# Two layers of a hybrid encoder on one core: the seven products of a pair of FFN slices are spread over a block of four slices

## The chip, the core and the metric

The kernel runs on one core of a Trainium2 chip. The core has a matrix engine (TensorE: PE for its matmuls, PEld for the loads of its stationary operand), VectorE (DVE), ScalarE (ACT), GpSimd (POOL) and SyncE (SP, which here only issues DMAs). Each engine works off its own queue in order. The metric is the device time of one execution in microseconds; lower is better. "us" is microseconds throughout.

## What is computed

Two layers, each of a half-step SwiGLU feed-forward network (FFN), a mixer, and a second FFN, on 256 tokens of width 1024 with `D_FF = 2816`:

```python
def swiglu(u, w_in, w_out):
    gate, up = jnp.split(u @ w_in, 2, axis=-1)
    return (jax.nn.silu(gate) * up) @ w_out

for l in range(DEPTH):
    h = swiglu(rmsnorm(x, ffn1_pre_g[l]), ffn1_w_in[l], ffn1_w_out[l])
    x = x + 0.5 * rmsnorm(h, ffn1_post_g[l])
    h = hybrid_mixer(rmsnorm(x, mix_pre_g[l]), ...)
    x = x + rmsnorm(h, mix_post_g[l])
    h = swiglu(rmsnorm(x, ffn2_pre_g[l]), ffn2_w_in[l], ffn2_w_out[l])
    x = x + 0.5 * rmsnorm(h, ffn2_post_g[l])
```

There are four FFNs, called FFN 1 to 4 here in order of time (layer 0: 1 and 2; layer 1: 3 and 4). FFN 2 is followed at once by FFN 3.

## The kernel before

**Precision.** Every fp32 operand is split into a high part (a cast to fp32r on ACT) and a low part (the remainder, a subtraction on DVE), and every product is three matmuls, hi·hi, lo·hi and hi·lo (`mm3`, L386 to L388). Each matmul is 128 x 128 by 128 x 512.

**Weights.** All weights come in one stream of units of 128 x 1024 in the order in which they are used (`Stream`). For each unit ACT writes `whi` (L153) and DVE writes `wlo` (L154). There are `WBUFS = 8` such pairs of buffers, so the splitting runs at most eight units ahead of the matmuls: unit n can be written when PE has read unit n - 8 for the last time. SP loads the raw weights, two units (1 MB) at a time into three `raw` buffers.

**FFN.** The inner width is cut into `NS = 11` slices of 256 columns. A *plain* slice is projected for both token blocks (`fin`, 2 x 24 matmuls on 4 units), passes silu and a product (`gate_up`, ACT L441, DVE L442), is transposed and split (`ftr`, L453, L371 and L372) and multiplied with its rows of the output weights (`fout`, 2 x 12 matmuls on 2 units). So PE stays 12 matmuls on every unit.

**Groups.** In FFN 2, 3 and 4 the slices (2, 3) and (6, 7) are projected as a *group* with seven products, P1 to P7, in place of eight (a Strassen-like scheme over token blocks and halves of the contraction). Each product is 12 matmuls on 2 units, so PE stays 6 matmuls on a unit. The operands of the products are made on DVE from the raw weights (`Stream.part`): for each group three subtractions or additions per quarter ahead of P6 (L175 to L177) and one ahead of P4 (L179), 16 in all of 128 x 512; and their results are combined on DVE (L487, L491, L492, L495, L496, L501, L512), 7 of 128 x 512. The raw weights of a group are eight loads of 0.5 MB into `gw` tiles (pool `spl`, 7 buffers) and `w4` tiles, which stay occupied until P5 and P4 have been split. A group's order in the code is

```python
product(s, "P1", lambda ps: act.copy(u, ps))
product(s, "P3", lambda ps: act.copy(v, ps))
product(s, "P2", first)
fout(s - 1, 0); fout(s - 1, 1)
product(s, "P6", sixth)
ftr(s, 0)
product(s, "P7", lambda ps: dve.tensor_add(w, u, ps))
product(s, "P5", fifth)
product(s, "P4", fourth)
fout(s, 0)
```

The results of projections and products go through two PSUM buffers (`psin`): a product can start when the one two before it has been read out. The accumulators of the output are `psacc`. The order on each engine is set by the scheduler of the framework when the kernel is built; it starts from the order of the code.

Of the kernel before, what the change touches and what calls it, by code (L numbers as in the profile page):

```python
# [53 lines left out]
P1 = _snap(TWO_PI, 2.0 ** -10)  # L54
P2 = _snap(TWO_PI - P1, 2.0 ** -23)
# [21 lines left out]


PRODUCTS = (("P1", 2), ("P3", 0), ("P2", 3), ("P6", 2), ("P7", 0), ("P5", 1), ("P4", 3))
GROUPS = (2, 6)  # L80


def ffn_plan(groups):

    r, s = [], 0
    while s <= NS:
        if s in groups:
            r += [("g1", s), ("out", s - 1), ("g2", s), ("out", s)]
            s += 2
            continue  # L90
        if s < NS:
            r.append(("in", s))
        if s >= 1:
            r.append(("out", s - 1))
        s += 1
    return r


MIXER_UNITS = 152
SIZE = {"in": 4, "out": 2, "g1": 6, "g2": 8}  # L100


def stream_plan():

    r = []
    for l in range(L):
        for f in range(2):
            for k, _ in ffn_plan(GROUPS if (l, f) != (0, 0) else ()):
                if k in ("in", "out"):
                    r += [None] * SIZE[k]  # L110
                else:
                    r += [(n, q, h) for n, q in (PRODUCTS[:3] if k == "g1" else PRODUCTS[3:]) for h in range(2)]
            if f == 0:
                r += [None] * MIXER_UNITS
    return r
# [89 lines left out]
def trunk_kernel(ctx: ExitStack, tc: tile.TileContext, x_in, pos, gains, gain0, par, id_in, consts, gw, w, out):  # L205
# [214 lines left out]
    def ffn(l, kpost, after, turn, during=None, start=False, fast=False):  # L420


        ui, uo, hT = {}, {}, {}
        groups = () if start else GROUPS
        for k, s in ffn_plan(groups):
            us = st.take(SIZE[k])
            if k == "out":
                uo[s] = us
            else:
                ui[s] = ui.get(s, []) + us  # L430
        acc = [ps_acc() for _ in range(NTB)]

        def fin(s, tb, turn=None):
            gate_up(s, tb, [inproj(ui[s], tb, turn)])

        def gate_up(s, tb0, pss):
            for tb, ps in enumerate(pss, tb0):
                t = tok()
                with tc.high_priority(offset=CHAIN_LEAD if s == NS - 1 else 0):
                    if fac[tb] is None:  # L440
                        act.activation(t[:, 0:256], ps[:, 0:256], AF.Silu)  # L441
                        dve.tensor_mul(t[:, 256:512], ps[:, 256:512], t[:, 0:256])  # L442
                    else:
                        act.activation(t[:, 0:256], ps[:, 0:256], AF.Silu, scale=fac[tb])
                        dve.scalar_tensor_tensor(t[:, 256:512], ps[:, 256:512], fac[tb], t[:, 0:256],
                                                 op0=ALU.mult, op1=ALU.mult)
                hT[(s, tb)] = t

        def ftr(s, tb):
            t = hT[(s, tb)]  # L450
            pt = ps_tr()
            for i in range(2):
                pe.transpose(pt[:, i * P:(i + 1) * P], t[:, 256 + i * P:256 + (i + 1) * P], ident)  # L453
            hl = tp.tile([P, 2, 256], F32R, tag=("tmp", "tok")[tb], name=nm("hl"), bufs=(TMP, TOK)[tb])
            with tc.high_priority(offset=CHAIN_LEAD if s == NS - 1 else 0):
                split(hl[:, 0, :], hl[:, 1, :], pt[:, 0:256])
            hT[(s, tb)] = hl

        def fout(s, tb, ns=(0, 1)):
            hl = hT[(s, tb)]  # L460
            outproj(acc[tb], [(hl[:, 0, c * P:(c + 1) * P], hl[:, 1, c * P:(c + 1) * P]) for c in range(2)],
                    uo[s], s == 0, s == NS - 1, ns)

        def product(s, n, use):

            ps = ps_in()
            i = [k for k, _ in PRODUCTS].index(n)
            us = ui[s][2 * i:2 * i + 2]
            for p in range(4):
                h, lo = st.get(us[p // 2])  # L470
                c = slice((p % 2) * 512, (p % 2 + 1) * 512)
                if n in ("P1", "P2", "P4"):
                    tb, k = {"P1": (0, 0), "P2": (0, 1), "P4": (1, 1)}[n]
                    ah, al = uh[tb][:, 2 * p + k, :], ul[tb][:, 2 * p + k, :]
                else:
                    k = ("P7", "P3", "P6", "P5").index(n)
                    ah, al = [v[:, k, p % 2, :] for v in sums[p // 2]]
                mm3(ps, ah, al, h[:, c], lo[:, c], p == 0, p == 3)
            use(ps)
            st.done(us)  # L480

        def group(s):

            (u, v), (z, w) = halves(w4()), halves(w4())

            def first(ps):
                dve.tensor_add(z, u, ps)  # L487
                gate_up(s, 0, [z])

            def sixth(ps):  # L490
                dve.tensor_add(u, u, ps)  # L491
                dve.tensor_add(v, v, u)  # L492

            def fifth(ps):
                dve.tensor_add(v, v, ps)  # L495
                dve.tensor_add(u, w, ps)  # L496
                gate_up(s + 1, 0, [v])
                gate_up(s + 1, 1, [u])

            def fourth(ps):  # L500
                dve.tensor_add(w, w, ps)  # L501
                gate_up(s, 1, [w])

            product(s, "P1", lambda ps: act.copy(u, ps))
            product(s, "P3", lambda ps: act.copy(v, ps))
            product(s, "P2", first)
            fout(s - 1, 0)
            fout(s - 1, 1)
            st.done(uo[s - 1])
            product(s, "P6", sixth)  # L510
            ftr(s, 0)
            product(s, "P7", lambda ps: dve.tensor_add(w, u, ps))  # L512
            product(s, "P5", fifth)
            product(s, "P4", fourth)
            fout(s, 0)
            ftr(s + 1, 0)
            ftr(s + 1, 1)
            ftr(s, 1)
            fout(s, 1)
            st.done(uo[s])  # L520

        st.fill()
        if start:
            gate_up(0, 0, inproj2(ui[0]))
            st.done(ui[0])
            fin(1, 0)
            ftr(0, 0)
        else:
            fin(0, 0)
            fin(1, 0, turn)  # L530
            ftr(0, 0)
            fin(0, 1)
            st.done(ui[0])
        ftr(1, 0)
        fin(1, 1)
        ftr(0, 1)
        st.done(ui[1])
        fout(0, 0)
        fout(0, 1)
        ftr(1, 1)  # L540
        st.done(uo[0])
        s = 1
        while s < NS - 2:
            s += 1
            if s == 4 and during is not None:
                during()
            if s in groups:
                group(s)
                s += 1
                continue  # L550
            fin(s, 0)
            fin(s, 1)
            st.done(ui[s])
            fout(s - 1, 0)
            ftr(s, 0)
            fout(s - 1, 1)
            ftr(s, 1)
            st.done(uo[s - 1])
        e = NS - 1

        def tail(tb):
            fin(e, tb)
            fout(e - 1, tb, (0,))
            ftr(e, tb)
            fout(e - 1, tb, (1,))

        tail(0)
        fout(e, 0)
        with tc.high_priority(offset=CHAIN_LEAD):
            post(0, acc[0], l, kpost, 0.5)  # L570
            turn = after(0)
        tail(1)
        st.done(ui[e])
        st.done(uo[e - 1])
        fout(e, 1, (0,))
        if turn is not None:
            turn()
        fout(e, 1, (1,))
        st.done(uo[e])
        with tc.high_priority(offset=CHAIN_LEAD):  # L580
            post(1, acc[1], l, kpost, 0.5, fast)
            return after(1)
# [516 lines left out]
    return list(wm.reshape(-1, P, D))  # L1099


def _ffn_units(w_in, w_out, groups):
    r = []
    o = _out_units(w_out)

# [1 line left out]
        c = np.arange(s * 256, (s + 1) * 256)  # L1107
        return np.concatenate([c, DFF + c])

    for k, s in ffn_plan(groups):  # L1110
        if k == "in":
            r += _in_units(w_in, cols(s))
        elif k == "out":
            r += o[2 * s:2 * s + 2]
        elif k == "g1":
            b = [w_in[:, cols(s + n)].reshape(KD, P, 512) for n in range(2)]
            for c in range(0, KD, 2):
                r += [np.concatenate([b[1][c + 1], b[1][c]], axis=1),
# [54 lines left out]
def _layout(i):  # L1173
    a = {n: np.asarray(v) for n, v in i.items()}
    units = []
    for l in range(L):
        units += _ffn_units(a["ffn1_w_in"][l], a["ffn1_w_out"][l], GROUPS if l > 0 else ())
        units += _mixer_units(a["w_mix_in"][l], a["w_lru_out"][l], a["w_ret_out"][l], a["w_sc_out"][l],
                              a["w_mix_out"][l])
        units += _ffn_units(a["ffn2_w_in"][l], a["ffn2_w_out"][l], GROUPS)  # L1180
    gains = [a[n][l] for l in range(L) for n in ("ffn1_pre_g", "ffn1_post_g", "mix_pre_g", "mix_post_g",
                                                 "ffn2_pre_g", "ffn2_post_g")]
    gains = np.stack([np.broadcast_to(g, (P, D)) for g in gains])
# [33 lines left out]
```

## Time and profile before

| | |
|---|---|
| time, median of 3 runs | 1685.47 us (1685.13 to 1686.81) |
| the profiled execution: its time, its span | 1687.89 us, 1686.1 us |
| PE busy, matmuls | 1658.7 us (98%), 7577 |
| PEld busy | 1361.0 us (81%) |
| DVE busy | 1205.7 us (72%) |
| ACT busy | 910.1 us (54%) |
| DMA, mean | 184 GB/s |

Busy time counts an engine's instructions from start to end; matmuls overlap one another, so a PE that is busy all the time can still be slower than it could be. Better are the starts of successive matmuls and the granted clock of TensorE. FFN 2 lies at 655 to 847 us of the span, FFN 3 at 847 to 1037, FFN 4 at 1491 to 1679.

### The profile page before, as it was taken

What the parts mean: (1) busy time and instruction counts of PE and PEld (TensorE: products, weight loads), DVE (VectorE), ACT (ScalarE), POOL (GpSimd) and SP (SyncE); (2) the same over time, 40 slices, a digit from 0 to 9 for tenths busy, and PEclk for the clock granted to TensorE, in tenths of its full rate; (3) what the DMA queues carried; (4) which work ended last, traced back from release to release, by engine and by line L of the source; (5) the groups of instructions that cost most, each with busy time, mean ns of one, the idle gap of its engine ahead of it and who ended that gap; (6) DMA issues with size and microseconds to landing.
All of it is one profiled execution on the core that took longest, in us unless ns stands there. A gap on an engine that the chain in (4) does not pass through costs nothing.

```text
span 1686.1 us, 19900 instructions
## 1 busy us (share of the span) xinstructions
PE 1658.7 (98%) x7577; PEld 1361.0 (81%) x7577; DVE 1205.7 (72%) x1629; ACT 910.1 (54%) x1335; POOL 65.0 (4%) x110
## 2 busy tenths in 40 slices
PE   9999999999999999999999999999999999999998
PEld 7888788888888887787787887888888888877886
DVE  6655669956656657978598866799666556589783
ACT  6444577644545455656465545766445445466552
POOL 0300100000000001000000001000000000010000
PEclk9999999999999999999999999999999999999999
DMA  8554454555444556446456164545554444745341
GB/s 309 209 196 178 175 187 166 210 186 200 169 180 160 184 220 219 148 182 212 163 199 213 75 233 167 203 171 200 194 189 166 172 178 164 260 175 182 131 175 50
DMA packets 48623, 309.86 MB, mean 184 GB/s; under 512 B 5520, under 2 KB 5904, under 8 KB 15376
## 3 DMA queue, kind: packets, MB, share of 16 engines
q1 hardware_dynamic: 46224, 301.18, 48.9%
q10 hardware_dynamic: 2304, 7.41, 1.3%
q8 instruction: 59, 0.97, 0.2%
q14 instruction: 36, 0.29, 0.0%
HBM read 307.52 MB, written 1.05 MB: 183 GB/s over the span
## 4 chain that ended last, share of the span: by engine, by line
PE 88%; DVE 8%; issue 1%; DMA 1%; POOL 1%; ACT 1%; DVEq 0%; POOLq 0%; ACTq 0%
PE psin L386 20%; PE psin L387 20%; PE psin L388 20%; PE psacc L388 8%; PE psacc L387 8%; PE psacc L386 8%; DVE wlo L154 5%; PE pstr L453 1%; PE pstr L696 1%; DMA raw<-in_w_dram 1%; PE pstr L348 1%; POOL small L292 1%; PE pstr L861 1%; DVE gw L176 0%; DVE gw L175 0%
## 5 line engine op out<-in xcount | busy, mean ns | idle before, releaser
L154 DVE TENSOR_TENSOR wlo<-raw,whi 128x1024 fp32r<-128x1024 f32 (+1 forms) x522 | 625.3, 1215 | 289.9 <-ACT whi L153 278.6
L153 ACT CAST whi<-raw 128x1024 fp32r<-128x1024 f32 (+1 forms) x522 | 536.3, 1049 | 250.2 <-PE psacc L388 128.0
L386 PE MATMUL psin<-whi,uh 128*128 128x512 f32 x1480 | 584.3, 395 | 1.9 <-ACT whi L153 1.4
L388 PE MATMUL psin<-whi,ul 128*128 128x512 f32 x1480 | 578.6, 391 | 2.2 <-DVE ul L372 2.2
L387 PE MATMUL psin<-wlo,uh 128*128 128x512 f32 x1480 | 580.0, 392 | 0.4 <-DVE wlo L154 0.4
L388 PEld LDWEIGHTS psin<-whi,ul 128*128 128x128 f32 x1480 | 278.2, 188 | 60.4 <-DVE ul L372 3.1
L386 PEld LDWEIGHTS psin<-whi,uh 128*128 128x128 f32 x1480 | 278.4, 188 | 57.7 <-ACT whi L153 1.8
L387 PEld LDWEIGHTS psin<-wlo,uh 128*128 128x128 f32 x1480 | 278.4, 188 | 55.7 <-DVE wlo L154 1.1
L386 PE MATMUL psacc<-whi,hl 128*128 128x512 f32 x352 | 141.3, 403 | 9.1 <-ACT whi L153 9.1
L388 PE MATMUL psacc<-whi,hl 128*128 128x512 f32 x352 | 137.6, 394 | 1.0 <-DVE hl L372 1.0
L387 PE MATMUL psacc<-wlo,hl 128*128 128x512 f32 x352 | 137.1, 391 | 0.0
L386 PE MATMUL psacc<-whi,spl 128*128 128x512 f32 x256 | 100.1, 391 | 0.0
L388 PE MATMUL psacc<-whi,spl 128*128 128x512 f32 x256 | 99.6, 389 | 0.0
L387 PE MATMUL psacc<-wlo,spl 128*128 128x512 f32 x256 | 99.6, 389 | 0.0
L292 POOL TENSOR_SCALAR small<-small 128x1 f32<-128x1 f32 x39 | 27.5, 705 | 1568.2 <-ACT w L287 1567.5
L386 PEld LDWEIGHTS psacc<-whi,hl 128*128 128x128 f32 x352 | 66.3, 189 | 23.4 <-ACT whi L153 10.4
L154 DVE TENSOR_TENSOR wlo<-gw,whi 128x512 fp32r<-128x512 f32 x120 | 76.8, 681 | 9.5 <-ACT whi L153 9.2
L388 PEld LDWEIGHTS psacc<-whi,hl 128*128 128x128 f32 x352 | 66.0, 188 | 17.8 <-DVE hl L372 4.2
L153 ACT CAST whi<-gw 128x512 fp32r<-128x512 f32 x120 | 68.0, 620 | 22.2 <-DVE gw L179 9.7
L387 PEld LDWEIGHTS psacc<-wlo,hl 128*128 128x128 f32 x352 | 66.3, 188 | 12.8
L371 ACT CAST hl<-pstr 128x256 fp32r<-128x256 f32 x88 | 32.5, 370 | 69.4 <-PE pstr L453 69.3
L684 ACT COPY tok<-psin 128x512 f32<-128x512 f32 x40 | 23.5, 587 | 62.6 <-PE psin L388 62.6
(191 smaller groups left out, 1645.8 us busy)
## 6 DMA issues: line engine op xcount, KB each, us to landing
raw<-in_w_dram SPq DMA_DIRECT2D x259, 1024.0 KB, 4.9
gw<-in_w_dram SPq DMA_DIRECT2D x36, 512.0 KB, 7.0
w<-in_w_dram SPq DMA_DIRECT2D x12, 512.0 KB, 4.7
gain<-in_gains_dram ACTq DMA_DIRECT2D x10, 512.0 KB, 4.5
w<-in_gw_dram ACTq DMA_DIRECT2D x4, 512.0 KB, 3.4
x<-in_x_dram SPq DMA_DIRECT2D x2, 512.0 KB, 4.9
raw<-in_w_dram SPq DMA_DIRECT2D x4, 256.0 KB, 6.0
out_dram<-x SPq DMA_DIRECT2D x4, 256.0 KB, 2.0
```

Of the source, the lines that this page charges most:

```text
L153: nc.scalar.copy(hi[:, k:k + n], raw)
L154: nc.vector.tensor_sub(lo[:, k:k + n], raw, hi[:, k:k + n].bitcast(F32))
L292: first_e.tensor_scalar(r, ss[:, 0:1], more, EPS / (f * f), op0=ALU.add, op1=ALU.add)
L348: pe.transpose(pt[:, i * P:(i + 1) * P], t[:, c * P:(c + 1) * P], ident)
L371: act.copy(h, src)
L386: pe.matmul(ps, lhsT=xh, rhs=wh, start=first, stop=False)
L387: pe.matmul(ps, lhsT=xh, rhs=wl, start=False, stop=False)
L388: pe.matmul(ps, lhsT=xl, rhs=wh, start=False, stop=last)
L453: pe.transpose(pt[:, i * P:(i + 1) * P], t[:, 256 + i * P:256 + (i + 1) * P], ident)
L684: act.copy(t, ps)
L696: pe.transpose(pt[:, i * SEQ + tb * P:i * SEQ + (tb + 1) * P], toks[tb][:, c * P:(c + 1) * P], ident)
L861: pe.transpose(pt[:, i * P:(i + 1) * P], qk[:, i * P:(i + 1) * P], ident)
```

## The change

Slices 2 to 5 and 6 to 9 become blocks (a, b, c, d). Slices a and b are projected plainly, c and d with the seven products, and the products stand between the steps of a and b. There are still two groups of seven products in each of FFN 2, 3 and 4, so the number of instructions on every engine stays as it was. What moves is the order, that of the weights in the stream with it. `during` (one load of a gain) moves from ahead of slice 4 to ahead of slice 6 in FFN 3.

```diff
-GROUPS = (2, 6)
+SLOT = dict(PRODUCTS)
+BLOCKS = ((2, 3, 4, 5), (6, 7, 8, 9))
...
-        if s in groups:
-            r += [("g1", s), ("out", s - 1), ("g2", s), ("out", s)]
-            s += 2
+        block = [b for b in blocks if b[0] == s]
+        if block:
+            a, b, c, d = block[0]
+            r += [("in", a), ("P1", c), ("out", a - 1), ("P3", c), ("P2", c), ("in", b), ("P6", c), ("out", a),
+                  ("P7", c), ("out", b), ("P5", c), ("P4", c), ("out", c)]
+            s += 4
             continue
...
-            product(s, "P1", lambda ps: act.copy(u, ps))
-            product(s, "P3", lambda ps: act.copy(v, ps))
-            product(s, "P2", first)
-            fout(s - 1, 0)
-            fout(s - 1, 1)
-            st.done(uo[s - 1])
-            product(s, "P6", sixth)
-            ftr(s, 0)
-            product(s, "P7", lambda ps: dve.tensor_add(w, u, ps))
-            product(s, "P5", fifth)
-            product(s, "P4", fourth)
-            fout(s, 0)
-            ftr(s + 1, 0)
-            ftr(s + 1, 1)
-            ftr(s, 1)
-            fout(s, 1)
-            st.done(uo[s])
+            fin(a, 0)
+            fin(a, 1)
+            st.done(ui[a])
+            product(c, "P1", lambda ps: act.copy(u, ps))
+            fout(a - 1, 0)
+            ftr(a, 0)
+            fout(a - 1, 1)
+            ftr(a, 1)
+            st.done(uo[a - 1])
+            product(c, "P3", lambda ps: act.copy(v, ps))
+            product(c, "P2", second)
+            fin(b, 0)
+            fin(b, 1)
+            st.done(ui[b])
+            product(c, "P6", sixth)
+            fout(a, 0)
+            ftr(b, 0)
+            fout(a, 1)
+            ftr(b, 1)
+            st.done(uo[a])
+            product(c, "P7", lambda ps: dve.tensor_add(w, u, ps))
+            ftr(c, 0)
+            fout(b, 0)
+            fout(b, 1)
+            st.done(uo[b])
+            product(c, "P5", fifth)
+            product(c, "P4", fourth)
+            fout(c, 0)
+            ftr(d, 0)
+            ftr(d, 1)
+            ftr(c, 1)
+            fout(c, 1)
+            st.done(uo[c])
...
-            if s == 4 and during is not None:
+            if s == (4 if start else 6) and during is not None:
                 during()
-            if s in groups:
-                group(s)
-                s += 1
+            if any(b[0] == s for b in blocks):
+                block(*range(s, s + 4))
+                s += 3
                 continue
```

The built programs show where things stand. In the rows below the number right behind `whi` or `wlo` is that of the weight unit; `s_` tiles are the summed activations, `hl_` is a slice ready for its output product. All rows are of the first group or block of FFN 2.

On PE of the kernel before, the end of P7 (units 238 and 239) and what follows: two matmuls of the output product of slice 2 (unit 244), then P5 (units 240 and 241).

```order
L386 MATMUL psin_491_5743<-whi239_5637,s_459_5385 128x512
L387 MATMUL psin_491_5743<-wlo239_5638,s_459_5385 128x512
L388 MATMUL psin_491_5743<-whi239_5637,s_460_5386 128x512
L386 MATMUL psacc_444_5307<-whi244_5729,hl_490_5740 128x512
L386 MATMUL psacc_445_5308<-whi244_5729,hl_490_5740 128x512
L386 MATMUL psin_492_5767<-whi240_5660,s_455_5369 128x512
```

On PE of the changed kernel, the end of P7 (units 248 and 249): a transposition and the output product of slice 3 (unit 250) follow.

```order
L389 MATMUL psin_505_5947<-wlo249_5853,s_459_5385 128x512
L390 MATMUL psin_505_5947<-whi249_5852,s_460_5386 128x512
L452 MATMUL pstr_506_5971<-ident_70,tok_495_5777 128x128 x2
L388 MATMUL psacc_444_5307<-whi250_5860,hl_502_5910 128x512
L389 MATMUL psacc_444_5307<-wlo250_5861,hl_502_5910 128x512
```

Between P7 and P5 there were two matmuls, and P5 followed P6 after 12 matmuls of P7 and these; now 24 matmuls of slice 2's output, P7 and 24 of slice 3's output lie between P6 and P5.

On DVE of the kernel before, the combination after P6 (L491, reading `psin_488`) and what stands around it: the operands of P4 are made (L179) and split (units 242 and 243) ahead of it.

```order
L179 TENSOR_TENSOR w4_471_5461<-w4_471_5461 128x512
L154 TENSOR_TENSOR wlo242_5699<-gw_467_5447,whi242_5698 128x512
L154 TENSOR_TENSOR wlo242_5699<-gw_469_5451,whi242_5698 128x512
L179 TENSOR_TENSOR w4_473_5465<-w4_473_5465 128x512
L154 TENSOR_TENSOR wlo243_5707<-w4_471_5461,whi243_5706 128x512
L491 TENSOR_TENSOR w4_482_5577<-w4_482_5577,psin_488_5712 128x512
L154 TENSOR_TENSOR wlo244_5730<-raw119_5727,whi244_5729 128x1024
```

On DVE of the changed kernel the same combination (L489, reading `psin_500`):

```order
L181 TENSOR_TENSOR w4_479_5525<-w4_479_5525 128x512
L156 TENSOR_TENSOR wlo250_5861<-raw124_5858,whi250_5860 128x1024
L441 TENSOR_TENSOR tok_499_5843<-psin_498_5818,tok_499_5843 128x256
L156 TENSOR_TENSOR wlo251_5865<-raw124_5858,whi251_5864 128x1024
L489 TENSOR_TENSOR w4_482_5573<-w4_482_5573,psin_500_5868 128x512
L156 TENSOR_TENSOR wlo252_5884<-gw_472_5505,whi252_5883 128x512
```

It now stands behind the splits of slice 3's output weights (units 250 and 251), and P4's splits (units 254 and 255) come after it.

On SP of the changed kernel, the loads of the second block's products (into the buffers that P5 and P4 of the first block give free); `raw127` holds units 260 and 261, the last ahead of P1 of the second block (units 262 and 263), `raw132` units 264 and 265:

```order
L136 DMA raw127_6032<-in_w_dram 128x2048
L170 DMA gw_514_6061<-in_w_dram 128x1024
L170 DMA gw_515_6063<-in_w_dram 128x1024
L170 DMA gw_516_6065<-in_w_dram 128x1024
L170 DMA gw_517_6073<-in_w_dram 128x1024
L170 DMA w4_518_6075<-in_w_dram 128x1024
L170 DMA gw_519_6077<-in_w_dram 128x1024
L170 DMA w4_520_6079<-in_w_dram 128x1024
L136 DMA raw132_6129<-in_w_dram 128x2048
```

On SP of the kernel before, the same seven loads stand between `raw121` (units 248 and 249) and `raw122` (units 250 and 251), four pairs of plain weights ahead of P1 of the second group (units 258 and 259):

```order
L134 DMA raw121_5788<-in_w_dram 128x2048
L168 DMA gw_512_5991<-in_w_dram 128x1024
...
L168 DMA w4_518_6009<-in_w_dram 128x1024
L134 DMA raw122_5815<-in_w_dram 128x2048
L134 DMA raw123_5867<-in_w_dram 128x2048
```

The loads now come last ahead of the P1 that needs them. Between P4 of one group and P1 of the next lie the weights of one output slice and one plain slice (6 units), where there were two plain slices and three output slices (14 units).

## Rows read from the trace of the kernel before

**Rows 1.** The page: busy time, share of the span, instructions by engine.

```profile
PE 1658.7 (98%) x7577; PEld 1361.0 (81%) x7577; DVE 1205.7 (72%) x1629; ACT 910.1 (54%) x1335; POOL 65.0 (4%) x110
```

**Rows 2.** Waits of PE over the span: total us, times, longest us.

```profile
PE psacc L386 <- ACT whi L153: 9.1, 3, 3.1
...
PE pstr L453 <- DVE tok L442: 2.1, 2, 1.1
...
PE pstr L453 <- DVE hl L372: 0.7, 1, 0.7
```

**Rows 3.** Timeline of PE: P6 to P7's end in group 1, FFN 2, then the clock.

```profile
701.73 0.39 PE L388 MATMUL psin<-whi,s 128*128 128x512 f32 x1
...
704.71 0.39 PE L388 MATMUL psin<-whi,s 128*128 128x512 f32 x1
708.16 0.73 PE L386 MATMUL psacc<-whi,hl 128*128 128x512 f32 x2 [3.06 <-ACT whi L153]
...
711.08 0.63 PE L388 MATMUL psin<-whi,s 128*128 128x512 f32 x1
711.51 0.63 PE L386 MATMUL psin<-whi,s 128*128 128x512 f32 x1
```

**Rows 4.** Timeline of PE: first and last matmul of P6, group 2, FFN 2.

```profile
769.85 0.39 PE L386 MATMUL psin<-whi,s 128*128 128x512 f32 x1
...
772.34 0.39 PE L388 MATMUL psin<-whi,s 128*128 128x512 f32 x1
```

**Rows 5.** Busy time by stretch: two groups of FFN 2, 3 and 4.

```profile
core 0: us, PE busy (x) PEld busy (x) DVE busy (x) ACT busy (x) POOL busy (x), PEclk, DMA share, GB/s
...
688.40:719.10 30.70, 27.01 (x112) 21.47 (x111) 30.70 (x49) 17.38 (x28) 0.00 (x0) 0.94 0.53 189
759.00:784.00 25.00, 25.00 (x111) 20.26 (x110) 25.00 (x40) 16.10 (x26) 0.00 (x0) 1.00 0.63 214
879.20:910.00 30.80, 27.61 (x110) 21.79 (x109) 30.80 (x49) 17.36 (x28) 0.00 (x0) 0.89 0.57 192
950.30:975.40 25.10, 25.10 (x112) 20.30 (x111) 25.10 (x40) 16.32 (x28) 0.00 (x0) 1.00 0.27 90
1524.20:1555.00 30.80, 27.66 (x110) 21.82 (x109) 30.80 (x49) 17.37 (x28) 0.00 (x0) 0.89 0.54 191
1595.20:1620.40 25.20, 25.20 (x112) 20.38 (x111) 25.20 (x40) 16.35 (x28) 0.00 (x0) 1.00 0.27 89
```

**Rows 6.** The same columns: plain slice 4, entry of FFN 2, group 1 with its backlog.

```profile
739.20:756.10 16.90, 16.90 (x79) 13.89 (x78) 12.31 (x22) 8.04 (x17) 0.00 (x0) 1.00 0.13 53
655.90:682.00 26.10, 25.17 (x117) 20.54 (x118) 22.67 (x39) 15.98 (x31) 2.95 (x4) 1.00 0.67 236
682.00:720.90 38.90, 35.21 (x151) 28.23 (x150) 38.87 (x60) 23.81 (x40) 0.00 (x0) 0.96 0.46 167
```

**Rows 7.** Timeline of DVE: three shapes back to back, the combination L491.

```profile
650.19 5.76 DVE L154 TENSOR_TENSOR wlo<-raw,whi 128x1024 fp32r<-128x1024 f32 x5
...
682.98 2.49 DVE L154 TENSOR_TENSOR wlo<-gw,whi 128x512 fp32r<-128x512 f32 x4
...
708.79 0.67 DVE L491 TENSOR_TENSOR w<-w,psin 128x512 f32<-128x512 f32 x1
...
724.07 0.75 DVE L372 TENSOR_TENSOR hl<-pstr,hl 128x256 fp32r<-128x256 f32 x2
...
774.73 0.67 DVE L491 TENSOR_TENSOR w<-w,psin 128x512 f32<-128x512 f32 x1
```

**Rows 8.** Timeline of ACT: the cast of unit 244, and a wait behind group 2.

```profile
705.34 1.17 ACT L153 CAST whi<-gw 128x512 fp32r<-128x512 f32 x2 [1.45 <-DVE gw L179]
...
707.07 1.99 ACT L153 CAST whi<-raw 128x1024 fp32r<-128x1024 f32 x2
...
786.65 2.00 ACT L153 CAST whi<-raw 128x1024 fp32r<-128x1024 f32 x2 [2.86 <-DMA raw<-in_w_dram]
```

**Rows 9.** A stretch in which the DMA engines are nearly full (columns of Rows 5).

```profile
710.00:712.00 2.00, 2.00 (x8) 1.53 (x7) 2.00 (x4) 1.69 (x3) 0.00 (x0) 0.60 0.93 295
```

More of the change, by code (lines that the diff above doesn't have):

```diff
@@ L79, with ffn_plan @@
 PRODUCTS = (("P1", 2), ("P3", 0), ("P2", 3), ("P6", 2), ("P7", 0), ("P5", 1), ("P4", 3))
-GROUPS = (2, 6)
-def ffn_plan(groups):
+SLOT = dict(PRODUCTS)
+BLOCKS = ((2, 3, 4, 5), (6, 7, 8, 9))
+def ffn_plan(blocks):
     r, s = [], 0
     while s <= NS:
-        if s in groups:
-            r += [("g1", s), ("out", s - 1), ("g2", s), ("out", s)]
-            s += 2
+        block = [b for b in blocks if b[0] == s]
[4 more added lines that the diff above has]
+            s += 4
             continue
@@ L99 @@
 MIXER_UNITS = 152
-SIZE = {"in": 4, "out": 2, "g1": 6, "g2": 8}
+SIZE = {"in": 4, "out": 2}
 def stream_plan():
@@ L107, in stream_plan @@
         for f in range(2):
[L108 to L112, printed above, removed]
+            for k, _ in ffn_plan(BLOCKS if (l, f) != (0, 0) else ()):
+                r += [(k, SLOT[k], h) for h in range(2)] if k in SLOT else [None] * SIZE[k]
             if f == 0:
@@ L420, in ffn @@
     def ffn(l, kpost, after, turn, during=None, start=False, fast=False):
[L423 to L430, printed above, removed]
+        ui, uo, up, hT = {}, {}, {}, {}
+        blocks = () if start else BLOCKS
+        for k, s in ffn_plan(blocks):
+            us = st.take(SIZE.get(k, 2))
+            {"in": ui, "out": uo}.get(k, up)[(k, s) if k in SLOT else s] = us
         acc = [ps_acc() for _ in range(NTB)]
@@ L466, in product @@
             ps = ps_in()
-            i = [k for k, _ in PRODUCTS].index(n)
-            us = ui[s][2 * i:2 * i + 2]
+            us = up[(n, s)]
             for p in range(4):
@@ L480, in product, with block, second @@
             st.done(us)
-        def group(s):
+        def block(a, b, c, d):
             (u, v), (z, w) = halves(w4()), halves(w4())
-            def first(ps):
+            def second(ps):
                 dve.tensor_add(z, u, ps)
-                gate_up(s, 0, [z])
+                gate_up(c, 0, [z])
             def sixth(ps):
@@ L496, in fifth @@
                 dve.tensor_add(u, w, ps)
-                gate_up(s + 1, 0, [v])
-                gate_up(s + 1, 1, [u])
+                gate_up(d, 0, [v])
+                gate_up(d, 1, [u])
             def fourth(ps):
                 dve.tensor_add(w, w, ps)
-                gate_up(s, 1, [w])
-            product(s, "P1", lambda ps: act.copy(u, ps))
-            product(s, "P3", lambda ps: act.copy(v, ps))
-            product(s, "P2", first)
-            fout(s - 1, 0)
-            fout(s - 1, 1)
-            st.done(uo[s - 1])
-            product(s, "P6", sixth)
-            ftr(s, 0)
-            product(s, "P7", lambda ps: dve.tensor_add(w, u, ps))
-            product(s, "P5", fifth)
-            product(s, "P4", fourth)
-            fout(s, 0)
-            ftr(s + 1, 0)
-            ftr(s + 1, 1)
-            ftr(s, 1)
-            fout(s, 1)
-            st.done(uo[s])
+                gate_up(c, 1, [w])
+            fin(a, 0)
[31 more added lines that the diff above has]
+            st.done(uo[c])
         st.fill()
@@ L1099, in _out_units, with _ffn_units @@
     return list(wm.reshape(-1, P, D))
-def _ffn_units(w_in, w_out, groups):
+def _ffn_units(w_in, w_out, blocks):
     r = []
@@ L1108, in cols @@
         return np.concatenate([c, DFF + c])
-    for k, s in ffn_plan(groups):
+    for k, s in ffn_plan(blocks):
         if k == "in":
@@ L1114, in _ffn_units @@
             r += o[2 * s:2 * s + 2]
-        elif k == "g1":
+        elif k == "P1":
             b = [w_in[:, cols(s + n)].reshape(KD, P, 512) for n in range(2)]
@@ L1176, in _layout @@
     for l in range(L):
-        units += _ffn_units(a["ffn1_w_in"][l], a["ffn1_w_out"][l], GROUPS if l > 0 else ())
+        units += _ffn_units(a["ffn1_w_in"][l], a["ffn1_w_out"][l], BLOCKS if l > 0 else ())
         units += _mixer_units(a["w_mix_in"][l], a["w_lru_out"][l], a["w_ret_out"][l], a["w_sc_out"][l],
                               a["w_mix_out"][l])
-        units += _ffn_units(a["ffn2_w_in"][l], a["ffn2_w_out"][l], GROUPS)
+        units += _ffn_units(a["ffn2_w_in"][l], a["ffn2_w_out"][l], BLOCKS)
     gains = [a[n][l] for l in range(L) for n in ("ffn1_pre_g", "ffn1_post_g", "mix_pre_g", "mix_post_g",
```

## The prediction

> **What bounds the kernel now.** I read the page first. PE is busy 98% of the span [rows 1], so the question is not which engine is the bound on the whole, but where PE runs below its pace. Its pace is 11 starts from 769.85 to 772.34 us, 0.2264 us for a matmul of 512 columns [rows 4]; the change removes no matmul, so only lost time can come back. The list of PE's waits comes next: the largest is three waits of 3.1 us, 9.1 us in all, each for a weight cast of ACT ahead of an output product [rows 2]. The timeline shows the first of them: P7 starts its last matmul at 704.71, the next one starts at 708.16, and some 2 us later matmuls start every 0.43 us in place of 0.23 [rows 3]. The granted clock is 0.94, 0.89 and 0.89 over the three stretches with such a wait and 1.00 over the three without [rows 5]: after the wait TensorE runs for some microseconds at 1.2 GHz in place of 2.4. So the wait is paid about twice.
>
> All three sit in the first group of their FFN, between P7 and P5. Who is late there? ACT's cast of unit 244 (707.07) comes directly after casts that waited for DVE's L179 [rows 8], and DVE is busy 38.87 of 38.90 us from 682.0 to 720.9 [rows 6]. It makes up a backlog: P6 starts its last matmul at 701.73 [rows 3], and DVE reads its result at 708.79 [rows 7], 7.1 us later. In the second group P6 starts its last matmul at 772.34 [rows 4] and is read at 774.73 [rows 7], 2.4 us later, and PE does not wait there, though DVE is busy all of these 25.0 us too [rows 5]. So inside a group DVE is the bound, and the look-ahead of eight units covers that once, unless DVE comes in late. It does at an FFN's entry, where it is busy 22.67 of 26.10 us [rows 6].
>
> **What DVE has to do, and PE in that time.** Prices by shape are 5.76/5 = 1.15 us for 1024 columns, 2.49/4 = 0.62 for 512 and 0.75/2 = 0.37 for 256 [rows 7]. A group needs 28 half-unit splits, 16 operand steps and 7 combinations, 51 x 0.62 = 31.6; four splits of output units, 4.6; eight of 256 columns, 3.0: 39.2 us. PE needs 132 matmuls x 0.2264 = 29.9, and four pairs of transpositions at 0.3 (an estimate: the 25.00 us of FFN 2's second group less 109 x 0.2264 leave 0.3 for its one pair [rows 5]), 31.1 us. DVE falls 8.1 us behind in every group, and gains in plain slices, where it is busy 12.31 of 16.90 us [rows 6].
>
> A block of four has the same 51 steps (31.6), 16 splits of plain units (18.4) and 16 of 256 columns (5.9): 55.9 us. PE has 276 matmuls (62.5) and eight pairs (2.4): 64.9 us. DVE is at 86% over the block and no longer behind. That an average fits does not say that its parts do, so I took the two halves from the order of the changed kernel. From the start of P1 to that of P6, PE has 108 matmuls and two pairs, 25.1 us; the DVE instructions from the first split of P2's units to the last of P6's are 5 of 1024, 20 of 512 and 4 of 256 columns, 5.8 + 12.4 + 1.5 = 19.7 us. From P6 to the P1 of the next block PE has 174 matmuls and six pairs, 41.2 us; DVE 9, 26 and 8, 10.4 + 16.1 + 3.0 = 29.5 us. Both fit, by 5 and by 11 us.
>
> The place of the wait itself: P5 writes the PSUM buffer that P6 wrote, so it needs the combination after P6. Between P6's last split and that combination stand 15 DVE instructions before (14 x 0.62 + 0.37 = 9.1 us) and 13 now (3 x 1.15 + 8 x 0.62 + 2 x 0.37 = 9.2 us). From P6's start to P5's PE had 24 matmuls (5.4 us) and the two that were pulled forward; now it has 72 and three pairs, 17.2 us. The need is the same and the time three times as long. What is late next there is nothing by the same count: P7 has 62 matmuls (14 us) after its buffers come free for 4.4 us of splits and operand steps, P4 has 50 (11.3 us) for some 3 us.
>
> **Part by part.** (1) The three waits and the slow stretches behind them go. The first and the second group of an FFN hold the same matmuls. In FFN 2 the second takes 25.00 us for 111, so the 112 of the first should take 25.2 us and took 30.7: 5.5 us. In FFN 3, 110 x 25.10/112 = 24.7 against 30.8: 6.1 us; in FFN 4, 110 x 25.20/112 = 24.8 against 30.8: 6.0 us [rows 5]. Together 17.6 us. (2) Matmuls, splits and operand steps: none added or removed, 0. (3) The wait of 0.7 us behind group 2 of FFN 2 [rows 2]: ACT's in-order queue stood 2.86 us at 786.65 for a raw load [rows 8], which was queued behind six loads of product weights for FFN 3. The same six loads stand now behind P4 of FFN 2's second block, ahead of the weights of the output product of slice 9, whose cast stands on ACT ahead of the silu of P5. By the stretch with 295 GB/s [rows 9], five of them that wait for P4's splits and the raw pair behind them are 3.7 MB, 12.4 us; PE has 58 matmuls, 13.1 us, until it needs that silu's turn. That is a margin of nothing. I take the 0.7 us as it is now (net 0), with bounds of 0 and of ACT's whole 2.9 us. (4) Between the blocks, seven loads follow raw127 on SP, and raw132 waits behind them. Six wait for P4's splits and are 3.1 MB, 10.7 us at 295 GB/s; the last is cast on ACT ahead of the silu after P4, and from P4's splits to P4's end PE has 60 matmuls and two pairs, 14.2 us. Covered by 3 us; if that cover went, the silu and the transposition behind it would wait for the rest, three times, 0 to 2.9 us each by the ACT row. (5) Ends of FFNs: two waits for `tok`, 2.1 us [rows 2], stand in the same order of instructions now as before: 0. (6) The load of a gain ahead of slice 6 is on ACT's queue, used after slice 10: 0.
>
> Sum: 17.6 us. The profiled execution took 1687.9 us, which makes 1670.3; it stands 2.4 us above the median of the runs, 1685.5, so the forecast for the median is **1668**.
>
> One rule bears on the size. By busy time alone PE lost 30.7 - 27.0 = 3.7, 3.2 and 3.1 us in the three stretches, 10.0 us [rows 5]. The Trainium skill (Perfetto Trace Analysis, Identifying the Most-Contended Engine) says that matmul busy time does not tell the distance to the limit, and to look at the busy share of weight loads. In the plain slice that is 13.89/16.90 = 82% [rows 6], in the three stretches 70, 71 and 71% [rows 5]: by it 4.6, 4.2 and 4.2 us are lost, 13 us in all, 1672 for the median. The trace agrees that busy time says too little; the count of starts, which I use, sees the slow clock whole.
>
> A second one bears on the range. The slow clock lasts longer after the second and third wait than after the first, though the waits are alike (6.1 and 6.0 against 5.5 us lost). The Trainium skill (TensorE: Matmul & The Clock Gate, Part 1: The HAM clock gate) calls the number of slow matmuls variable from run to run; no run here shows that yet. By it the three would lose 16.5 to 18.3 us, 1667 to 1669.
>
> **The rivals.** *Small waits remain or come up* (the DMA margins of 3 and 4, or a chain of add, silu and transposition that is short by little). For it: the margin in (3) is nil, and DVE enters the first block as late as before. Against it: the halves of the block fit by 5 and 11 us. Price: waits like the 0.7 to 1.1 us that the trace has elsewhere [rows 2], after which the clock stayed at 1.00, in six blocks, 4 to 7 us; up to half the gain, 9 us. It gives 1672 to 1677.
>
> *The wait moves with the products* in the first block of each FFN, because the backlog comes from the entry. Then the same 5.5 to 6.1 us stay and the time is 1685. Against it: a plain slice now stands between entry and P1, with 4 units in 10.9 us of PE, about 3 us of free DVE.
>
> *Slower:* the look-ahead. While PE works on a plain slice it holds its four units 10.9 us long, so DVE may split only four units ahead and the operand steps of P6 (12 x 0.62 = 7.4 us, with P6's and the plain slice's splits 14.5 us) come too late in all six blocks. It decides from the point where they don't start before P3's end: PE has 60 matmuls there, 13.6 us, less than 14.5. Then each block pays a wait with a slow clock, 5.8 us x 6 = 35, less 17.6: 1703. Against it: the operand steps need only splits of P3 and P2, and no free unit buffer, so they can run while PE is still on P1 to P2.
>
> That the change does not do what it says is excluded by the order of the built program.
>
> **How the numbers follow.** Forecast (all three waits gone, no new one above 1 us each) 0.68; small waits 0.18; wait moved 0.06; slower 0.08. A measurement of this kernel can tell about 0.2%, 3.4 us, from no change. Faster 0.86, same 0.06, slower 0.08. The range goes from 1664 (18.3 us, the 0.7 us and the spread of the runs shown, 1.7 us) to 1677 (small waits at their largest) and leaves out the two last rivals.
>
> **What would show it.** In the trace after: no wait of PE for a weight cast of 3 us; granted clock 1.00 from 650 to 1680; DVE with gaps inside the blocks, about 86% busy; the combination after P6 read within 3 us of P6's last start. Step (3) is wrong if PE waits at the end of FFN 2 for the silu after P5; step (4) if it does so between blocks in all three FFNs. The forecast is wrong if a wait long enough to lower the clock appears in any block; its place (ahead of P6, or ahead of P5) would tell the look-ahead from the backlog.

## The result, and the profile after

The changed kernel takes 1666.37 us (median of 4 runs, 1666.25 to 1666.93). Beside it the kernel before took 1685.89 us (1685.13 to 1686.81): a ratio of 0.9885, 95% interval 0.9867 to 0.9902. That is 19.5 us or 1.15% less, far over the 0.2% that a measurement here can tell. The forecast was 1668, the range 1664 to 1677.

The page of after, busy time by engine (answers to [rows 1]) and the shares of the chain of work that ended last; below it the span with its mean granted clock:

```profile
PE 1646.6 (99%) x7577; PEld 1356.3 (81%) x7577; DVE 1204.4 (72%) x1629; ACT 914.0 (55%) x1335; POOL 65.0 (4%) x110
...
PE 92%; DVE 3%; ACT 1%; issue 1%; DMA 1%; POOL 1%; DVEq 0%; POOLq 0%; ACTq 0%
```

```profile
core 0: 1664.4 us, clock 0.998
```

The numbers of instructions are those of before, on every engine; the span is 21.7 us shorter than the 1686.1 us of before. The largest waits of PE in after (total us, times, longest us; answers to [rows 2]):

```profile
PE psin L388 <- ACT whi L155: 2.3, 1, 2.3
PE psin L390 <- DVE ul L374: 2.2, 2, 1.1
PE pstr L452 <- DVE tok L441: 2.0, 2, 1.0
```

The three waits for a weight cast ahead of an output product, 9.1 us in [rows 2], are gone from the list, and so is the 0.7 us for `hl`; the two of 1.0 us for `tok` at the ends of FFNs are left. The first row is the start of the program.

The blocks by stretch (columns of [rows 5]): FFN 2's first and second block, the first block of FFN 3 and of FFN 4, then the two halves of FFN 2's first block, P1 to P6 and P6 to the next P1:

```profile
684.50:747.10 62.60, 62.60 (x286) 51.64 (x284) 53.41 (x81) 37.74 (x62) 0.00 (x0) 1.00 0.55 201
747.10:812.00 64.90, 64.90 (x295) 53.19 (x293) 55.10 (x83) 38.25 (x60) 0.00 (x0) 1.00 0.52 187
868.10:931.40 63.30, 63.30 (x288) 52.22 (x287) 54.10 (x82) 37.71 (x62) 0.00 (x0) 1.00 0.55 199
1506.50:1569.80 63.30, 63.30 (x288) 52.22 (x287) 54.11 (x82) 37.71 (x62) 0.00 (x0) 1.00 0.55 198
695.80:720.70 24.90, 24.90 (x114) 20.53 (x112) 24.83 (x39) 15.45 (x25) 0.00 (x0) 1.00 0.36 127
720.70:762.00 41.30, 41.30 (x189) 33.76 (x188) 31.61 (x49) 24.53 (x42) 0.00 (x0) 1.00 0.63 229
```

PE has no gap in any of them and the granted clock is 1.00 throughout, where [rows 5] has 0.94, 0.89 and 0.89. DVE is busy 85% of a block.

**Where the time came from.** I laid the starts of all matmuls of the two traces side by side. The region that the change orders anew begins with the first matmul of slice 2 and holds 552 matmuls of 512 columns and 16 pairs of transpositions in both (in before it ends at the first matmul of slice 10). That region took 136.5, 136.1 and 136.1 us in FFN 2, 3 and 4 and takes 129.35, 129.34 and 129.37: 20.6 us. The way to the first of them took 1.0 us less, and each of the stretches between and behind them stands within 0.15 us. Against 0.2266 us for an undisturbed start, the 20.6 us are, roughly: 13.8 us of starts over 0.25 us late (the waits of [rows 2], which count idle time alone, and the late starts directly behind them), 5.0 us of starts at the slow clock, 1.2 us of slightly late starts just behind transpositions and 1.1 us of them elsewhere, less 0.5 us that transpositions take longer.

### The profile page after: what moved, and what is told of

Same layout as the page of the kernel before. It is cut to its first block, busy times and chain, and to the rows that moved or that the text cites. A ratio compares the mean times of both kernels' runs of the same rounds, so it can differ in the third digit from the quotient of the medians.

```text
span 1664.4 us, 19878 instructions
## 1 busy us (share of the span) xinstructions
PE 1646.6 (99%) x7577; PEld 1356.3 (81%) x7577; DVE 1204.4 (72%) x1629; ACT 914.0 (55%) x1335; POOL 65.0 (4%) x110
## 4 chain that ended last, share of the span: by engine, by line
PE 92%; DVE 3%; ACT 1%; issue 1%; DMA 1%; POOL 1%; DVEq 0%; POOLq 0%; ACTq 0%
PE psin L388 20%; PE psin L390 20%; PE psin L389 20%; PE psacc L390 9%; PE psacc L388 9%; PE psacc L389 9%; DVE wlo L156 1%; PE pstr L452 1%; DMA raw<-in_w_dram 1%; PE pstr L710 1%; POOL small L294 1%; PE pstr L350 1%; PE pstr L875 1%; ACT w L289 0%; PE pstr L947 0%
```

## The experiments

**The theory** of the prediction: DVE is late in the first group of an FFN because it falls behind in a dense group and comes in late already; spreading the products gives it room. **Rival A** is that distance from the FFN's entry is what counts (a plain slice ahead of the first block), spreading nothing. **Rival B** is that density alone counts, wherever the group stands. **Rival C** puts the wait down to the order of DVE's queue, not to its amount. The look-ahead as a limit on the new order is a fourth question.

**Distance without spreading.** The dense groups of before, begun later:

```diff
-GROUPS = (2, 6)
+GROUPS = (4, 8)
```

> The kernel before with its two dense groups moved from slices (2, 3) and (6, 7) to (4, 5) and (8, 9), the slices that have the products in the changed kernel; nothing is spread. Theory A (DVE enters the first group late from the FFN's entry; one group alone fits the look-ahead): two plain slices ahead of the group let DVE catch up, no wait of 3 us is left, 17 to 18 us are gained, 1667 to 1670 us. Theory B (the density of a group itself is what costs, only spreading helps): a wait of about 3 us with a slow clock stays in a group of each FFN, 1684 to 1687 us.

Measured 1671.23 us (1670.58 to 1671.85), ratio 0.9909 [0.9893, 0.9926]; that is 1.2 us above the range for distance alone. No wait of 3 us is left and the clock is 0.998. Rival B falls: dense groups alone don't make the waits. Of 19.5 us distance gives 15.5. What is left is small and lies partly outside the groups:

```profile
PE psin L387 <- DVE wlo L154: 1.0, 3, 0.6
PE pstr L348 <- DVE w L312: 0.6, 2, 0.5
...
PE pstr L453 <- DVE hl L372: 0.5, 1, 0.5
```

Starts are 0.61 and 0.77 us late at the entries of the next FFN and the mixer, in waits for DVE; I read them as the backlog of the second group, which now stands close to the FFN's end. The row for `hl` is one wait behind the first group of FFN 3. And each FFN keeps some 0.4 us of slightly late starts that after doesn't have.

**How much distance?** Two more places for the dense groups. In the first of them the second change keeps the load of a gain, which stood at slice 4, ahead of the first group:

```diff
-GROUPS = (2, 6)
+GROUPS = (3, 7)
...
-            if s == 4 and during is not None:
+            if s == (4 if start else 3) and during is not None:
```

> The kernel before with its groups begun at slices 3 and 7 in place of 2 and 6: one more plain slice ahead of the first group, and the groups still dense; the load of a gain stays ahead of the first group. Theory (the backlog comes from the entry and a plain slice works off 16.9 less 12.3 = 4.6 us of it): with P6's combination 7.1 us late in the first group and 2.4 us late in the second, a difference of 4.7 us, one more plain slice brings the first group to where the second was. The three waits of 3 us go, and the time is 1670 to 1675. Rival (two plain slices are needed, as ahead of the groups at 4 and 8): a wait of 1 us or more stays in the first group of each FFN, and the time is 1676 to 1683.

Measured 1671.01 us (1669.38 to 1671.35), ratio 0.9904 [0.989, 0.9919]. One more plain slice is enough for the large waits; the theory's range holds it, and a second one adds nothing. In FFN 2 and 4 one wait each is left, behind the first group, of the kind that before had behind FFN 2's second (the 0.7 us for `hl` in [rows 2]). The longer one, timeline of PE in FFN 4 (start, length, idle before and its releaser):

```profile
1561.96 0.44 PE L453 MATMUL pstr<-ident,tok 128*128 128x128 f32 x2 [1.30 <-DVE hl L372]
1562.15 0.48 PE L388 MATMUL psin<-whi,ul 128*128 128x512 f32 x1
1562.47 0.40 PE L386 MATMUL psin<-whi,uh 128*128 128x512 f32 x1
```

Then the same with the room taken from between the groups:

```diff
-GROUPS = (2, 6)
+GROUPS = (5, 8)
```

> The kernel before with its groups begun at slices 5 and 8: three more plain slices ahead of the first group, but one alone, in place of two, between the first and the second. A group puts DVE 8.1 us behind, by my count, and a plain slice gives 4.6 us back. Theory (what counts is the backlog at a group's start, whatever it comes from): the second group starts with some 3.5 us of backlog, waits of 1 to 3 us come up in it, in each FFN, and the time is 1674 to 1685. Rival (only the entry of an FFN leaves a backlog that matters; the look-ahead covers a group afresh each time): no wait over 1 us in the second group, and the time is that of the groups at 4 and 8, 1669 to 1673.

Measured 1674.63 us (1674.22 to 1675.83), ratio 0.9927 [0.9911, 0.9944], some 3 us above the groups at 4 and 8. Waits are back in the second group of all three FFNs, at the place where the first group of before had them, between P7 and P5. PE in FFN 2:

```profile
803.60 0.73 PE L386 MATMUL psacc<-whi,hl 128*128 128x512 f32 x2 [0.49 <-ACT whi L153]
804.35 0.50 PE L386 MATMUL psin<-whi,s 128*128 128x512 f32 x1
...
808.15 0.50 PE L388 MATMUL psacc<-whi,hl 128*128 128x512 f32 x1 [0.34 <-DVE hl L372]
```

The last of these lines is a wait between P5 and P4. The waits ahead of P5 are 0.5 us and not the 1 to 3 that I had worked out, so the count of the backlog is right in direction and too large. The longest wait stands elsewhere, behind the first group of FFN 3:

```profile
PE pstr L453 <- DVE hl L372: 1.5, 1, 1.5
```

The time lies in the theory's range, at its lower end, but the rival's condition, no wait over 1 us in the second group, holds too. What falls is the rival's reason, that the entry alone counts: a group leaves a backlog of its own, which one plain slice doesn't quite clear.

**Spreading without distance.** After, with P1, P3 and P2 put ahead of the block's first plain slice, and P6 between its two plain slices:

```diff
-            fin(a, 0)
-            fin(a, 1)
-            st.done(ui[a])
             product(c, "P1", lambda ps: act.copy(u, ps))
...
             product(c, "P2", second)
+            fin(a, 0)
+            fin(a, 1)
+            st.done(ui[a])
+            product(c, "P6", sixth)
...
-            product(c, "P6", sixth)
```

> The changed kernel with the products of a block ahead of its first plain slice: P1, P3 and P2 come directly behind the FFN's entry as in the kernel before, the two plain slices stand between P2 and P6 and between P6 and P7. Theory A alone (distance from the entry is what counts): the waits come back in the first block of each FFN, though they stand ahead of P6 now, 3 us and a slow clock each, 1680 to 1686 us. Spreading alone (DVE needs 19.7 us from P1 to P6 where PE has 25.1): no wait, 1665 to 1668 us.

Measured 1666.85 us (1666.13 to 1667.83), ratio 0.9883 [0.9868, 0.9897]: the time of after, without a wait in a block. So rival A falls too as the only cause. Either remedy takes the large waits away; spreading also takes the small ones.

**What DVE is late with.** The kernel before without the twelve steps of each group that make P6's, P7's and P5's operands (L175 to L177). These sums are left out of the computation:

```diff
-                dve.tensor_sub(b[0], b[0], b[1])
-                dve.tensor_sub(b[1], b[1], b[2])
-                dve.tensor_add(b[2], b[0], b[2])
+                pass
```

> The kernel before without the 12 operand steps of P6 per group on DVE (L175 to L177 are left out, the products P6, P7, P5 and P4 then use unsummed weights). Backlog on DVE: 12 x 0.62 = 7.4 us less per group, as much as the 7.1 us by which the combination after P6 was late, so the three waits go, 1665 to 1669 us. If the wait came from the output matmuls that the scheduler pulled ahead of P5 (they wait for the cast of unit 244), it stays, 1684 to 1687 us.

Measured 1668.68 us (1668.13 to 1669.95), ratio 0.9894 [0.9879, 0.9909]. The stretch that was 30.70 us long at a clock of 0.94 [rows 5], in this kernel:

```profile
688.40:719.10 30.70, 30.70 (x140) 24.93 (x139) 28.64 (x44) 18.98 (x32) 0.00 (x0) 1.00 0.79 278
```

140 matmuls in place of 112, and DVE no longer full. 7.4 us less work on DVE takes the three waits away: a backlog on DVE is their cause. (These steps also feed casts on ACT, so this run alone doesn't tell a full DVE from casts that wait for one step. DVE without a gap in [rows 5], and the DVE combination that comes late under the doses below, speak for the full DVE.)

**Order or amount?** The kernel before, with the two additions after P6 put first in DVE's queue:

```diff
-                dve.tensor_add(u, u, ps)
-                dve.tensor_add(v, v, u)
+                with tc.high_priority(offset=CHAIN_LEAD):
+                    dve.tensor_add(u, u, ps)
+                    dve.tensor_add(v, v, u)
```

> The kernel before with the two DVE additions after P6 given priority: they stand directly behind the splits of P7's units, ahead of P4's operand steps, and P5 comes ahead of the output matmuls of unit 244 on PE. Amount of DVE work: what was late stays late in sum, a wait of 2 to 3 us shows up ahead of the next weights (units 242 to 244), 1680 to 1686 us. Order of DVE's queue: the cast of unit 244 ended at about 708 us, and PE with P5 ahead of it wants it at 704.9 + 2.7 = 707.6, so 0.5 us of wait is left and no slow clock, 1667 to 1672 us.

Measured 1689.03 us (1688.26 to 1690.64), ratio 1.0017 [1.0008, 1.0027]. P5 now goes ahead of the output matmuls, and the same lateness meets those, in three pieces:

```profile
709.29 0.73 PE L386 MATMUL psacc<-whi,hl 128*128 128x512 f32 x2 [1.90 <-ACT whi L153]
711.19 0.73 PE L387 MATMUL psacc<-wlo,hl 128*128 128x512 f32 x2 [1.16 <-DVE wlo L154]
713.26 0.79 PE L388 MATMUL psacc<-whi,hl 128*128 128x512 f32 x1 [1.34 <-DVE hl L372]
713.85 0.63 PE L386 MATMUL psacc<-whi,hl 128*128 128x512 f32 x1
714.28 0.63 PE L387 MATMUL psacc<-wlo,hl 128*128 128x512 f32 x1
```

Rival C falls; it is the amount. That it became slower than before, by 0.2%, no theory had said: the range for the amount was 1680 to 1686.

**An inconclusive one.** The kernel before with the transposition of the group's first slice behind P5 in the code, to keep the output matmuls from being drawn ahead of P5:

```diff
-            ftr(s, 0)
             product(s, "P7", lambda ps: dve.tensor_add(w, u, ps))
             product(s, "P5", fifth)
+            ftr(s, 0)
             product(s, "P4", fourth)
```

> The kernel before with the transposition ftr(s, 0) behind P5 in the code, so that no output matmul of slice s can be pulled ahead of P5. If the pulled matmuls cause the wait, it goes and 1667 to 1670 us come out. If DVE's backlog does, P5 waits for the combination after P6 at the same time as before (about 709.5 us in FFN 2), and 1684 to 1688 us come out.

Measured 1691.20 us (1690.28 to 1691.82), ratio 1.0028 [1.0017, 1.0038]. The edit didn't do what it was meant to: two output matmuls still stand ahead of P5, and their waits are unchanged. So it says nothing on its question. Its new waits, three of 1.1 us in the second groups (L511 here is L512 of before, the combination after P7), show only how near to its edge that group was:

```profile
PE psacc L386 <- ACT whi L153: 9.3, 3, 3.1
PE psin L386 <- DVE w L511: 3.2, 3, 1.1
```

**How much margin has after?** DVE steps that change nothing (an addition and its inverse), put behind each making of operands, 8 and then 16 to a block, 4.8 and 9.6 us of DVE:

```diff
+                for _ in range(1):
+                    dve.tensor_add(b[0], b[0], b[1])
+                    dve.tensor_sub(b[0], b[0], b[1])
```

> The changed kernel with 8 more DVE steps of 128 x 512 ahead of P6 in each block (an operand is added back and subtracted again; 4.9 us by 0.61 each). If the halves of a block fit by 5 and 11 us as worked out, PE does not wait, 1665 to 1669 us. If a block has no slack (the look-ahead lets DVE start P6's steps only behind P3), six blocks lose 4 to 5 us each, 1690 us or more.

Measured 1670.68 us (1670.15 to 1671.32), ratio 0.991 [0.9895, 0.9925]: 1.7 us above the range for no wait, far from the 1690 for no slack. The second dose has `range(2)`:

> The same with 16 more steps (9.8 us) in each block. Slack of 5 us ahead of P6 and 11 us behind: 4 to 5 us too much ahead of P6 in each of six blocks, with the slow clock behind waits of 3 us, 1690 to 1710 us. If DVE could take what it misses from the second half (11 us free), no wait, 1665 to 1670 us.

Measured 1708.50 us (1708.3 to 1709.22), ratio 1.0135 [1.012, 1.015]. One row of each list of waits, 8 steps and then 16:

```profile
PE psin L391 <- DVE w L488: 1.4, 6, 0.3
```

```profile
PE psin L391 <- DVE w L488: 26.7, 6, 4.5
```

Six waits, one in each block, for the combination after P2 (L488 here, L485 in after). It frees the PSUM buffer that the second projection of the block's second plain slice writes. With 16 steps in FFN 2, the timeline of PE:

```profile
720.19 0.80 PE L391 MATMUL psin<-whi,uh 128*128 128x512 f32 x1 [4.46 <-DVE w L488]
720.78 0.63 PE L392 MATMUL psin<-wlo,uh 128*128 128x512 f32 x1
721.21 0.63 PE L393 MATMUL psin<-whi,ul 128*128 128x512 f32 x1
```

On DVE all 8 steps of the first dose start ahead of L488, and 15 of the 16 of the second, 0.60 us each. So 4.8 us of added work less waits of 0.3 us leave a margin of 4.5, and 9.0 less 4.5 leave 4.5 too. The first half of a block has some 4.5 us of room, ahead of this combination. Past it the cost is steep, since the clock falls with it (starts 0.43 us apart in the lines above): the second dose's 4.8 us cost 37.8 us in six blocks.

**The look-ahead.** After with six buffers for split units in place of eight:

```diff
-WBUFS = 8
+WBUFS = 6
```

> The changed kernel with six pairs of unit buffers in place of eight. If the look-ahead is what carries the blocks, waits of 2 us and more come up ahead of P6 or P1 in the blocks of FFN 2, 3 and 4, 1685 us or more. If DVE's balance carries them, the blocks stay free of waits over 1 us and the time stays within 1666 to 1675 us.

Measured 1697.53 us, in a single run. Neither outcome that I had written down came: blocks have no wait over 0.4 us, yet the time is far above 1675; it is lost at the FFNs' entries and in the mixers (from the end of FFN 3's steps to FFN 4, 453.1 us in after, 462.4 now). The two largest rows of its waits:

```profile
PE psin L389 <- DVE wlo L156: 14.7, 18, 2.4
PE pstr L350 <- DVE w L314: 4.9, 5, 1.3
```

So in this run the blocks don't hang on the look-ahead, and the rival that feared for it found nothing; the FFNs' entries and the mixers do hang on it. More buffers than eight weren't tried. None of these kernels is faster than after; the one with P1, P3 and P2 ahead of the plain slice equals it. A third group or block to an FFN wasn't tried.

## Why the prediction was right

**What bounds the kernel**: right. The waits were DVE's backlog: less work on DVE takes them away, reordering it doesn't, and a free slice ahead of the group does as well. The prediction named both sources, the dense group and the late entry, and did not say which is enough to remove. Either is: with distance alone the groups at 3 and 7 have no 3 us wait, with spreading alone the early block has none.

**(1) The three waits and the slow clock, 17.6 us**: right in kind, under-sized; the region lost 20.6 us of its time. The step priced the first group against the second, and the second was itself not clean. By starts against 0.2266 us the three first groups lost 6.0, 6.6 and 6.6 us, some 1.6 more than priced; 1.3 of that is what the three second groups lose in their own stretches, some 0.45 us each. Then, in FFN 2, the start at 790.15 was followed by one that came 0.84 us late, the wait for `hl` of [rows 2], which went (below). The rest are slightly late starts in the plain slices behind the groups. The yardstick should have been the pace of [rows 4], which stood in the prediction's first paragraph.

The profiled run of after took 1666.25 us, 4.1 below the 1670.3 of the sum: the 3.0 us of this step, and 1.0 us ahead of slice 2 of FFN 2, where nothing was changed. This 1.0 us is luck and no gain: FFN 2's first output matmul starts at 679.85 us in before and at 678.80 in after, and at 679.15 to 679.64 in the nine experiments with the same code up to there. Against that, I had taken off 2.4 us because the profiled run of before stood above its median; after's stands 0.1 below its own. The errors partly cancel, again by luck, so the median is 1.6 us off and not 4.

**(2) No work added**: right, by the counts of the page.

**(3) The wait behind FFN 2's second group, taken to stay**: wrong, on the good side. The margin was called nothing, and it was small; PE does not wait there. ACT, which stood 2.86 us for the load [rows 8], in after:

```profile
806.52 1.06 ACT L155 CAST whi<-raw 128x1024 fp32r<-128x1024 f32 x1 [0.30 <-PE psin L390]
807.48 0.72 ACT L440 ACTIVATE tok<-w 128x256 f32<-128x256 f32 x2
```

The cast waits 0.30 us, for a buffer that PE frees and no longer for the DMA, and the silu follows it at once. The 12.4 us for the loads had five of them, and the raw pair, behind one release. On SP's queue (start, us, how many) the six product loads stand from 789.39 for 6 us, and raw's begin at 799.51, 7 us ahead of the cast. By the order of loads and casts this first one is what the cast at 806.52 reads; by the trace it landed at 805.89, 0.6 us ahead:

```profile
789.39 6.00 SPq L170 DMA_DIRECT2D gw<-in_w_dram  x6
...
799.51 20.71 SPq L136 DMA_DIRECT2D raw<-in_w_dram  x5
```

**(4), (5) and (6)**: right. No wait stands between blocks in any FFN, and the two waits for `tok` are 2.0 us, as before 2.1.

**The balance of the halves**: the block's share was right (85% against 86%), the split of it wasn't what DVE does. From P1 to P6 it is busy 24.83 of 24.90 us, not 19.7 of 25.1: with room it works ahead, on what the second half needs, which is 31.61 us of 41.30. The two halves of the prediction's count don't make the whole either: 19.7 and 29.5 us of DVE are 49.2 where the block has 55.9, so its margins of 5 and 11 us were too wide against the block's 9.0. "Fits by 5 us" came near the 4.5 us that the doses found, in part by luck, since the prediction sought the place at the combination after P6. That one is read 0.4 us after P6's last start at 722.96 (7.1 us before [rows 3, 7]). What gives first is P2's:

```profile
709.89 0.68 DVE L485 TENSOR_TENSOR w<-w,psin 128x512 f32<-128x512 f32 x1
...
723.40 0.68 DVE L489 TENSOR_TENSOR w<-w,psin 128x512 f32<-128x512 f32 x1
```

**The two rules on the size.** Weight loads gave 13 us by their busy share for the three stretches; the starts give 19.2 there. The Trainium skill (Perfetto Trace Analysis, Identifying the Most-Contended Engine) is right that matmul busy time, 10.0 us here, says too little; of the three counts its own came second, and the starts themselves came nearest. On the slow clock: the stretches of before have 7, 9 and 10 matmuls that start 0.43 us apart, and those of the inconclusive experiment, at the same places, 9, 6 and 12 (two kernels, one trace of each). That agrees with what the Trainium skill (TensorE: Matmul & The Clock Gate, Part 1: The HAM clock gate) says of their number, that it varies. It moves the time by 1 us or so, and the range of 1667 to 1669 that came from it just missed the median.

**The rivals.** There were no small waits in the blocks. The wait did not move to the first block. The look-ahead's mechanism was not seen in the blocks, even with six buffers.

## What to carry to other kernels

When one engine runs at its limit for a stretch and is idle next to it, the gain is in letting it work ahead, by interleaving or by distance. The sum over the longer stretch (here 55.9 of 64.9 us) told that interleaving could work; a dose of idle work then shows the size of the margin and the place that gives first. Price a lost stretch against the clean pace of one instruction, not against a neighbouring stretch that may be losing too. And before writing a new order, try whether moving the old one by a slice or two gives most of it: the two numbers in `GROUPS` gave 15 of 19 us here.

## What the runs showed of the hardware

A wait's price depends on what stands near it. Alone, 1.30 us left the clock high (groups at 3 and 7): the matmuls behind 1561.96 start 0.23 to 0.32 us apart, and the granted clock is 1.00 from 1561 to 1570 us. Three of 1.90, 1.16 and 1.34 us with some matmuls between them were followed by starts 0.43 us apart (713.85, 714.28; two additions first in DVE's queue), at a granted clock of 0.50 from 713.8 to 718.0 us, which is 1.2 GHz in place of 2.4, as after one of 3.06 us [rows 3]. So splitting a wait into pieces close together saved nothing; the kernel with the three pieces in each of three groups took 3 us more than the one with the one wait. Why dense groups keep some 0.4 us of slightly late starts in each FFN that the spread ones lack (0.36 to 0.55 against 0.04) stays open.
